# The low part of the logits' products as pairs of half arrays in a stick-breaking attention layer

## The chip, the cores and the metric

The kernel runs on one core of one Trainium2 chip. The metric is the device time of one execution in microseconds (us). Before the change it is 3037.64 us, the median of 3 runs (3036.8 to 3038.7).

## What is computed

One encoder layer on a sequence of 2048 positions with 1024 channels, in float32: a norm, one projection into nine streams of 1024, an attention branch and a convolution branch with gates, a merge, an output projection and a norm at the end. The change lies in the attention: 16 heads of width 64.

```python
scale = 1.0 / math.sqrt(q.shape[-1])
logits = jnp.einsum('bqhd,bkhd->bhqk', qf[:, start:end], kf[:, :end])
mask = s_idx < t_idx
log_not_beta = jnp.where(mask, jax.nn.log_sigmoid(-logits), 0.0)
later = lax.cumsum(log_not_beta, axis=3, reverse=True) - log_not_beta
weights = jnp.where(mask, jnp.exp(jax.nn.log_sigmoid(logits) + later), 0.0)
outs.append(jnp.einsum('bhqk,bkhd->bqhd', weights, vf[:, :end]))
```

A query's weight on a key is the sigmoid of their logit times the product of one minus the sigmoid over all keys between the two.

## The kernel before

**Precision.** Each float32 product is made of float32r products over a split a = hi + lo (split, lines 112 to 114: ScalarE rounds to hi, VectorE subtracts). A projection takes three of them (line 194): hi times hi, hi times lo, lo times hi, over a contraction of 128. A head is only 64 wide, so the logits fit the array's 128 rows in another way: the queries' hi part stands twice in the tile qd, on partitions 0 to 63 and 64 to 127, and the tile k2 holds the keys' hi part on one half of the partitions and their lo part on the other. One product (line 572) gives q_hi k_hi + q_hi k_lo. A second one (line 573) adds q_lo k_hi: the tile ql holds q_lo on the partitions where k2 has the hi part, and zeros, set once at the start (line 512), on the other 64.

**Order of time.** The sequence is reversed, so a query r reads the keys s > r. The queries come in two halves of 1024: half 1 (whose queries have only the keys of their own half) is computed first, then half 0 (all keys). A head's queries go by 256 (a step's two tiles of 128 queries), from the last to the first. In half 1 a step's keys run from its first query to the end; in half 0 there are two steps for each 256 queries, one up to position 1024 (the diagonal piece) and one from there on. Within a step the keys are cut at chunks of 512: segments.

**A step's work.** The items of logits (lines 553 to 583, one for each tile and segment): two products into a PSUM tile lg, of which there are two (pool lgp), a sigmoid by ScalarE into the tile nb (line 575), and, when a tile's last segment is done, a running product along the keys by VectorE, a scan (line 578). Before, all segments of tile 0 come first, then those of tile 1. Then, for each 256 keys, a turn (line 601: TensorE transposes of nb against the identity, and a split into th and tl), and a product with the differences of the values (line 617), emitted two turns later.

**What sets the order.** TensorE executes in the order of emission; the other engines are ordered by the framework. weave_attention (line 643) lists the items of all heads: a logits item stands LEAD = 4 turns ahead of its share of its step's turns, but never more than one step ahead, since nb has NBW = 4 buffers, two for each step. Each item has a cost, an estimate in us of its time on TensorE (0.43 for a logits item of 512 columns), and emit_fill puts pieces of the projection stream (Fill, six products of 512 columns each, cost 1.3) between the items in proportion to the cost that has passed. After the attention, from about 2645 us on, only projections and the output remain.

**Transfers.** All run on the queue of SP. A head's loads are issued in one go by load, at its first logits item: qd (two DMAs for each chunk of queries), ql (one), k2 (two for each chunk of keys) and v2 (one). The weights' loads (line 148) and all others stand on the same queue, in order. The ring st of seven tiles of 128 x 512 stages what goes to and comes from DRAM. The tile dd, the first summand of the diagonal scans, holds the identity and zeros; ident is a tile of its own, and ones a full 128 x 128 tile.

Of the kernel before, what the change touches and what calls it, by code (L numbers as in the profile page):

```python
# [8 lines left out]
F32 = mybir.dt.float32  # L9
F32R = mybir.dt.float32r  # L10
AF = mybir.ActivationFunctionType
# [15 lines left out]
# The weave: buffers of weights, the lead of the logits, and distances and paces in pieces of the projection stream.  # L27
# [27 lines left out]
def layer_kernel(ctx: ExitStack, tc, x, w_in, w_sb, w_cv, w_out, vecs, cw, rows, out):  # L55
    """All sequences are reversed in time: row r is position S-1-r, so that a query r reads
    the keys s > r and the stick is broken in the direction of growing s.

    Every float32 product runs as float32r passes over an exact split a = hi + lo.

    The tensor engine runs in the order of emission: two streams, the attention and the
    projections, are woven so that what one waits for is covered by the other."""
# [5 lines left out]
    ident = const.tile([P, P], F32, name="ident")  # L68
    make_identity(nc, ident)
    ones = const.tile([P, P], F32, name="ones")  # L70
# [21 lines left out]
    def dma(dst, src):  # L92
        """A copy of bytes: float32r has float32's bits."""
        nc.sync.dma_start(out=dst.bitcast(F32) if dst.dtype == F32R else dst,
                          in_=src.bitcast(F32) if src.dtype == F32R else src)
# [20 lines left out]
    def negmean(mr):  # L116
        """-mean * rstd"""
        nm = sm.tile([P, 1], F32, name="nm")
        nc.gpsimd.tensor_scalar(out=nm, in0=mr[:, 0:1], scalar1=mr[:, 1:2], scalar2=-1.0, op0=ALU.mult, op1=ALU.mult)
        return nm  # L120
# [13 lines left out]
    def st(dt=F32):  # L134
        return sg_p.tile([P, CH], dt, name="st", tag="st", bufs=7)
# [4 lines left out]
    # -------------------------------------------------------------- projections, in pieces  # L140
    def load_w(src, col):
        """A block of 128 columns of a weight, [block, partition, kb, column], as hi and lo, contraction on the partitions."""
# [9 lines left out]
    class Fill:  # L152
        """The pieces of the projection stream: (cost in us of the tensor engine, emit)."""
# [21 lines left out]
        def parts(self, src, col, xs, use, *by):  # L175
            """A block: the pieces, per chunk, of out^T[col.., chunk] for each (chunk, acts) of xs; use(chunk, psum, ..) takes
            it, with what the loads `by` have brought. Also the item that loads the weights of the next block."""
# [43 lines left out]
        def pair(self, one, two, first=(), freed=((), ())):  # L221
            """Two blocks, the first chunk of both before the second of either. The items `first` run beside these
            pieces, freed[n] as the activations of chunk n are used up."""
# [28 lines left out]
    def prep(c):  # L252
        """The normed input of chunk c, transposed and split, into xt[c], in pieces."""
# [29 lines left out]
    def xa_tile(to, key):  # L283
        """The next block of a chunk's activations, hi and lo."""
        t = [xa.tile([P, CH], F32R, name=n, bufs=2 * KB) for n in ("xh", "xl")]
        hi, lo = to.setdefault(key, ([], []))
        hi.append(t[0])
        lo.append(t[1])
        return t
# [65 lines left out]
    def even_odd(t):  # L355
        """A row kept as its even and then its odd positions, in the order of the positions."""
        return t.rearrange("p (e n) -> p n e", e=2)

    def block_u(F, m, h):
        """u = c_val * sigmoid(c_gate) of a block of channels."""  # L360
# [23 lines left out]
    # -------------------------------------------------------------- causal depthwise convolution, norm over channels  # L384
# [3 lines left out]
    def conv(m, h, u):  # L388
        """y[r] = sum over d of t[d] u[r+d] + b, with t the taps reversed, on even and odd positions:
        y0 = t0 * (u0 - u1) + (t0 + t1) * u1,  y1 = t1 * (u0+ - u1) + (t0 + t1) * u1."""  # L390
# [39 lines left out]
    def conv_mean(h):  # L430
        """The means over the channels of half h, as items."""
        def mean(c):
# [3 lines left out]
            nc.tensor.matmul(ps, lhsT=ones, rhs=ysum[h][:, :, c % 2 * 256:c % 2 * 256 + 256], start=True, stop=True)  # L436
# [4 lines left out]
    def conv_ln(c):  # L441
        """The norm over the channels of chunk c, the swish and the gate of the branch, as items."""
# [58 lines left out]
    # -------------------------------------------------------------- attention, in items  # L501
    def attention(at, kv, lg_p, pv_p):
        """Summed by parts: with E[r, s] the product of 1 - sigmoid over the keys after r up to s, the weight of s is
        E[r, s-1] - E[r, s], so that o[r] = v[r] + sum over s >= r of E[r, s] (v[s+1] - v[s]), with v[S] = 0."""
        dd = at.tile([P, HALF], F32, name="dd", bufs=1)
        nc.gpsimd.memset(dd, 0.0)
        nc.vector.tensor_copy(out=dd[:, :P], in_=ident)
        sums = {}
        qlo = [[kv.tile([P, CH], F32R, name=f"ql{a}{n}", bufs=1) for n in range(2)] for a in range(2)]
        for a in range(2):  # L510
            for t in qlo[a]:
                nc.gpsimd.memset(t[64 - a * 64:128 - a * 64].bitcast(F32), 0.0)
        zero = at.tile([P, 1], F32, name="zero", bufs=1)
        nc.gpsimd.memset(zero, 0.0)

        def head(i, a, h):
            """The steps of head 2i+a for the queries of half h, each (L items, T/PV items)."""
            k2, v2, qd, ql = {}, {}, {}, {}
            chunks = half(h)

            def load():
                for c in chunks:
# [4 lines left out]
                    ql[c] = qlo[a][c % 2]  # L527
                    dma(ql[c][qs], qdr[c, i][1][qs])
                for c in ([1, 0, 2, 3] if h == 0 else [3, 2]):
                    k2[c] = kv.tile([P, CH], F32R, name="k2", bufs=8)  # L530
                    for e in range(2):
                        dma(k2[c][(a ^ e) * 64:(a ^ e) * 64 + 64], kdr[c, i][e][qs])
# [5 lines left out]
            for qc in (2 * chunks[0] + 1, 2 * chunks[0], 2 * chunks[1] + 1, 2 * chunks[1]):  # L538
# [3 lines left out]
                for pi, (lo, hi) in enumerate(pieces):  # L542
                    steps.append(make_step(i, a, qc, lo, hi, pi == 0, pi == len(pieces) - 1, k2, v2, qd, ql, po, prev,
# [3 lines left out]
        def make_step(i, a, qc, lo, hi, diag, last, k2, v2, qd, ql, po, prev, load):  # L547
# [5 lines left out]
            for j in range(2):  # L553
                s0 = lo + (j * P if diag else 0)
                segs = []
                s = s0
                while s < hi:
                    e = min(hi, (s // CH + 1) * CH)
                    segs.append((s, e))
                    s = e  # L560
                for n, (s, e) in enumerate(segs):
                    def fn(j=j, s0=s0, s=s, e=e, first=(n == 0), end=(n == len(segs) - 1)):
                        if load and first and j == 0:
                            load()
                        if first:
                            tiles[j] = at.tile([P, HALF], F32, name="nb", bufs=NBW)
                        nb = tiles[j]
                        w = e - s
                        kc, ko = s // CH, s % CH
                        js = slice(q * QW + j * P, q * QW + (j + 1) * P)  # L570
                        lg = lg_p.tile([P, CH], F32, name="lg")
                        nc.tensor.matmul(lg[:, :w], lhsT=qd[c][:, js], rhs=k2[kc][:, ko:ko + w], start=True, stop=False)  # L572
                        nc.tensor.matmul(lg[:, :w], lhsT=ql[c][:, js], rhs=k2[kc][:, ko:ko + w], start=False, stop=True)  # L573
                        o = s - s0
                        nc.scalar.activation(nb[:, o:o + w], lg[:, :w], AF.Sigmoid, scale=-QS)  # L575
                        if end:
                            w = hi - s0
                            nc.vector.tensor_tensor_scan(  # L578
                                out=nb[:, :w], data0=nb[:, :w], data1=dd[:, :w] if diag else zero.to_broadcast([P, w]),
                                initial=0.0 if diag else prev[j], op0=ALU.mult, op1=ALU.add)  # L580
                            if not last:
                                prev[j] = nb[:, w - 1:w]
                    items_l.append((0.43 * (e - s) / CH, fn))
# [59 lines left out]
    def weave_attention(steps):  # L643
        """The steps as one list of (cost, emit): the logits run ahead of the transposes, those of the products."""
# [25 lines left out]
    # -------------------------------------------------------------- branch projections, output  # L670
    acts = {}

    def load_acts(key, src, c):
        """The activations of chunk c, split where they land, as items."""
# [7 lines left out]
    def branch(n, h):  # L682
        """A gated branch of the merge for half h: of the attention into pdr, of the convolution into mdr."""
# [29 lines left out]
    def run(F, blks, freed):  # L713
        """The blocks of a half, by pairs at both ends so that one chunk's activations load beside the other's products."""
# [27 lines left out]
    def newest():  # L742
        """The newest instruction of the vector engine."""
# [21 lines left out]
    # -------------------------------------------------------------- the main phase  # L765
# [209 lines left out]
```

## Time and profile before

| what | value |
|---|---|
| median of 3 runs | 3037.64 us |
| span of the profiled execution | 3036.5 us |
| granted TensorE clock, mean | 0.996 |
| PE busy, matmuls | 2959.8 us, 15304 |
| ScalarE busy | 1269.5 us |
| logits, line 572, busy and mean | 246.4 us, 386 ns, 640 products |
| logits, line 573, busy and mean | 233.7 us, 366 ns, 640 products |
| DMA, mean | 150 GB/s |

The span runs from the first to the last instruction of one execution; the time of a run is about 1 us longer. PE is TensorE's matmuls and PEld its weight loads, which run beside them; DVE is VectorE, ACT ScalarE, POOL GpSimd, SPq the queue of SyncE. L573 is line 573 of the kernel. The busy time of PE counts overlapping matmuls with their full durations, and their ends are modelled, so the rate at which TensorE gets through its work is read from the distance of the starts. In a row of a group stand the count, the busy time, the mean in ns, and behind the second bar the idle time of the engine just before these instructions with what ended most of it. A row of the waits has who waited for whom, the total in us, the number of times and the longest. In the timeline a row has the start, the duration, the engine and the line.

### The profile page before, as it was taken

The page shows a single profiled execution, that of the slowest core. Times are in us where ns is not written, and L with a number is a line of the kernel's source. Part 1 is how long each engine was busy: PE and PEld are TensorE (multiplying, and loading weights), DVE is VectorE, ACT ScalarE, POOL GpSimd, SP SyncE. Part 2 cuts the span into 40 slices and gives each one's busy share as a digit, 9 for nine tenths or more (in the row PEclk, how much of TensorE's full clock was granted, in tenths as well). Part 3 has the DMA queues.
Part 4 walks back from the last instruction along what each step waited for, and adds up shares of the span by engine and source line. Part 5 has one row for each costly group of instructions (what it writes and reads, how often), then busy time and mean ns, then how long its engine had stood idle before and what let it go on. Part 6 is the DMA issues. An engine that isn't in the chain of part 4 may idle for free.

```text
span 3036.5 us, 41850 instructions
## 1 busy us (share of the span) xinstructions
PE 2959.8 (97%) x15304; PEld 2484.1 (82%) x15304; DVE 2381.6 (78%) x3175; ACT 1269.5 (42%) x2308; POOL 88.3 (3%) x178
## 2 busy tenths in 40 slices
PE   7999999999999999999999999999999999999998
PEld 6888888888887788888888888887888878878886
DVE  5587787777879888788879888879887788856656
ACT  5333333333336344444445444445445455533222
POOL 1000000000000000000000000000000000000000
PEclk9999999999999999999999999999999999999999
DMA  7543443434434533343335344335545666685552
GB/s 269 172 144 112 148 139 117 149 125 130 139 101 140 169 100 110 114 131 123 111 112 189 103 143 141 99 103 175 164 155 161 191 224 191 208 280 197 161 189 78
DMA packets 260221, 455.92 MB, mean 150 GB/s; under 512 B 30384, under 2 KB 55088, under 8 KB 259888
## 3 DMA queue, kind: packets, MB, share of 16 engines
q1 hardware_dynamic: 260016, 453.25, 46.0%
q8 instruction: 120, 1.97, 0.3%
q14 instruction: 85, 0.70, 0.1%
HBM read 292.70 MB, written 160.43 MB: 149 GB/s over the span
## 4 chain that ended last, share of the span: by engine, by line
PE 73%; DVE 11%; issue 10%; DMA 3%; ACT 2%; POOL 1%; SPq 0%; DVEq 0%; POOLq 0%; ACTq 0%
PE mm L194 52%; PE pv L617 7%; PE tp L601 6%; DVE nb L578 3%; PE lg L573 3%; PE lg L572 3%; DVE tl L114 2%; DVE wlo L114 1%; DVE cy L402 1%; PE mo L900 1%; DMA st<-ydq 1%; DMA ydq<-st 1%; DVE xl L114 1%; DVE st L494 0%; DVE st L493 0%
## 5 line engine op out<-in xcount | busy, mean ns | idle before, releaser
L194 PE MATMUL mm<-xh,whi 128*128 128x512 f32 x2816 | 1144.5, 406 | 1.7 <-ACT whi L113 1.5
L194 PE MATMUL mm<-xh,wlo 128*128 128x512 f32 x2816 | 1110.1, 394 | 1.4 <-DVE wlo L114 1.4
L194 PE MATMUL mm<-xl,whi 128*128 128x512 f32 x2816 | 1106.2, 393 | 1.2 <-DVE xl L114 1.2
L194 PEld LDWEIGHTS mm<-xh,wlo 128*128 128x128 f32 x2816 | 530.0, 188 | 120.9 <-DVE wlo L114 1.9
L194 PEld LDWEIGHTS mm<-xl,whi 128*128 128x128 f32 x2816 | 532.9, 189 | 86.8 <-DVE xl L114 2.4
L194 PEld LDWEIGHTS mm<-xh,whi 128*128 128x128 f32 x2816 | 531.5, 189 | 86.4 <-ACT whi L113 1.9
L113 ACT ACTIVATE th<-tp 128x512 fp32r<-128x512 f32 (+1 forms) x576 | 329.4, 572 | 613.9 <-PE tp L601 606.1
L114 DVE TENSOR_TENSOR tl<-tp,th 128x512 fp32r<-128x512 f32 (+1 forms) x576 | 376.5, 654 | 180.1 <-ACT th L113 178.2
L575 ACT ACTIVATE nb<-lg 128x512 f32<-128x512 f32 (+3 forms) x640 | 334.9, 532 | 308.9 <-PE lg L573 299.0
L578 DVE TENSOR_TENSOR_SCAN nb<-nb,dd 128x256 f32<-128x256 f32 (+7 forms) x256 | 345.1, 1350 | 42.2 <-ACT nb L575 41.5
L601 PE MATMUL tp<-ident,nb 128*128 128x128 f32 x2176 | 337.8, 274 | 20.3 <-DVE nb L578 18.2
L578 DVE TENSOR_TENSOR_SCAN nb<-nb,zero 128x1024 f32<-128x1024 f32 x128 | 300.0, 2346 | 36.5 <-ACT nb L575 36.2
L601 PEld LDWEIGHTS tp<-ident,nb 128*128 128x128 f32 x2176 | 263.4, 140 | 77.9 <-DVE nb L578 22.5
L113 ACT ACTIVATE whi<-wraw 128x512 fp32r<-128x512 f32 x352 | 217.6, 629 | 261.1 <-PE mm L194 238.8
L617 PE MATMUL pv<-tl,v 128*128 128x256 f32 (+1 forms) x1152 | 292.1, 282 | 12.2 <-DVE tl L114 11.6
L114 DVE TENSOR_TENSOR wlo<-wraw,whi 128x512 fp32r<-128x512 f32 x352 | 237.4, 682 | 80.0 <-ACT whi L113 52.9
L617 PE MATMUL pv<-th,v 128*128 128x256 f32 (+1 forms) x1152 | 299.5, 281 | 0.0
L572 PE MATMUL lg<-k,qd 128*128 128x512 f32 (+3 forms) x640 | 246.4, 386 | 11.6 <-ACT nb L575 7.0
L617 PEld LDWEIGHTS pv<-tl,v 128*128 128x128 f32 x1152 | 218.1, 189 | 36.4 <-DVE tl L114 17.2
L573 PE MATMUL lg<-k,ql 128*128 128x512 f32 (+3 forms) x640 | 233.7, 366 | 0.0
L617 PEld LDWEIGHTS pv<-th,v 128*128 128x128 f32 x1152 | 217.8, 189 | 18.5 <-issue 0.2
L402 DVE SCALAR_TENSOR_TENSOR cy<-cu,csum,cy 128x512 f32<-128x512 f32 x240 | 178.1, 742 | 4.4 <-ACT cy L398 0.9
(107 smaller groups left out, 2460.0 us busy)
## 6 DMA issues: line engine op xcount, KB each, us to landing
wraw<-in_w_in SPq DMA_DIRECT2D x288, 256.0 KB, 3.2
k<-kdr SPq DMA_DIRECT2D x192, 128.0 KB, 2.9
v<-vdr SPq DMA_DIRECT2D x96, 256.0 KB, 3.5
kdr<-st SPq DMA_DIRECT2D x64, 256.0 KB, 2.1
qdr<-st SPq DMA_DIRECT2D x64, 256.0 KB, 2.2
qd<-qdr SPq DMA_DIRECT2D x128, 128.0 KB, 2.8
vdr<-st SPq DMA_DIRECT2D x64, 256.0 KB, 2.0
xr<-in_x SPq DMA_DIRECT2D x32, 256.0 KB, 3.8
```

Source lines behind the costliest of these rows:

```text
L113: nc.scalar.activation(hi, src, AF.Copy)
L114: nc.vector.tensor_tensor(out=lo, in0=src, in1=hi.bitcast(F32), op=ALU.subtract)
L194: nc.tensor.matmul(box["ps"], lhsT=l[:, kb], rhs=r[kb], start=(kb == 0 and n == 0), stop=(kb == KB - 1 and n == 2))
L402: nc.vector.scalar_tensor_tensor(out=dst, in0=src[:, j:j + HN], scalar=t, in1=first, op0=ALU.mult, op1=ALU.add)
L572: nc.tensor.matmul(lg[:, :w], lhsT=qd[c][:, js], rhs=k2[kc][:, ko:ko + w], start=True, stop=False)
L573: nc.tensor.matmul(lg[:, :w], lhsT=ql[c][:, js], rhs=k2[kc][:, ko:ko + w], start=False, stop=True)
L575: nc.scalar.activation(nb[:, o:o + w], lg[:, :w], AF.Sigmoid, scale=-QS)
L578: nc.vector.tensor_tensor_scan(out=nb[:, :w], data0=nb[:, :w], data1=dd[:, :w] if diag else zero.to_broadcast([P, w]), initial=0.0 if diag ...
L601: nc.tensor.transpose(out=tp[:, at_:at_ + P], in_=tiles[j][:, so:so + P], identity=ident)
L617: nc.tensor.matmul(o[:, :w], lhsT=lv, rhs=tt[:, o0:o0 + w], start=(diag and t == 0 and n == 0 and e == 0), stop=(last and t == nt - 1 and ...
L900: nc.tensor.matmul(ps, lhsT=a[kb][:, js], rhs=b[:, kb, qs], start=(kb == 0 and n == 0), stop=(kb == KB - 1 and n == 2))
```

## The change

The second product of the logits drops its zero rows. For a segment, the two tiles of queries (j = 0 and 1) are now handled by one item: the first products of both, into both lg tiles; then the second products of both, each over 64 partitions only, tile 0 on one half of the array's rows and tile 1 on the other; then both sigmoids, and, at the step's last segment, both scans. For this, both halves need the keys' hi part: k2 has it on one half of the partitions, and a new tile kx gets it on the other, one tile kx for two chunks (which of the halves is which alternates with the chunk). ql shrinks to the two tiles' columns, packed, each on its half; it is loaded by two DMAs, and needs no zeros. Besides, the ring st has 6 tiles instead of 7, ident becomes the first 128 columns of dd, and ones one column that the one matmul that needs it broadcasts. A logits item has the cost 0.7 for 512 columns of both tiles, where the two items before had 0.86. Comments are dropped.

```diff
-    ident = const.tile([P, P], F32, name="ident")
+    dd = const.tile([P, HALF], F32, name="dd")
+    ident = dd[:, :P]
     make_identity(nc, ident)
-    ones = const.tile([P, P], F32, name="ones")
+    nc.gpsimd.memset(dd[:, P:], 0.0)
+    ones = const.tile([P, 1], F32, name="ones")
...
-        return sg_p.tile([P, CH], dt, name="st", tag="st", bufs=7)
+        return sg_p.tile([P, CH], dt, name="st", tag="st", bufs=6)
...
+        def half_of(a, e, c):
+            x = a ^ e ^ (c % 2)
+            return slice(x * 64, x * 64 + 64)
...
-                    ql[c] = qlo[a][c % 2]
-                    dma(ql[c][qs], qdr[c, i][1][qs])
+                    ql[c] = kv.tile([P, 2, P], F32R, name="ql", bufs=4)
+                    for j in range(2):
+                        dma(ql[c][half_of(a, j, c)], qdr[c, i][1][qs].rearrange("p (q j n) -> p q j n", q=2, j=2)[:, :, j])
...
+                    if c ^ 1 not in kx:
+                        kx[c] = kx[c ^ 1] = kv.tile([P, CH], F32R, name="kx", bufs=4)
                     for e in range(2):
-                        dma(k2[c][(a ^ e) * 64:(a ^ e) * 64 + 64], kdr[c, i][e][qs])
+                        dma(k2[c][half_of(a, e, c)], kdr[c, i][e][qs])
+                    dma(kx[c][half_of(a, 1, c)], kdr[c, i][0][qs])
...
-                        nc.tensor.matmul(lg[:, :w], lhsT=qd[c][:, js], rhs=k2[kc][:, ko:ko + w], start=True, stop=False)
-                        nc.tensor.matmul(lg[:, :w], lhsT=ql[c][:, js], rhs=k2[kc][:, ko:ko + w], start=False, stop=True)
...
+                lgs = [lg_p.tile([P, CH], F32, name="lg") for j in range(2)]
+                for j in range(2):
+                    nc.tensor.matmul(lgs[j][:, :e - ss[j]], lhsT=qd[c][:, q * QW + j * P:q * QW + (j + 1) * P],
+                                     rhs=k2[kc][:, ss[j] - kc * CH:e - kc * CH], start=True, stop=False)
+                for j in range(2):
+                    rows_ = half_of(a, j, c)
+                    kh = k2 if j ^ c % 2 == kc % 2 else kx
+                    nc.tensor.matmul(lgs[j][:, :e - ss[j]], lhsT=ql[c][rows_, q],
+                                     rhs=kh[kc][rows_, ss[j] - kc * CH:e - kc * CH], start=False, stop=True)
...
-                    items_l.append((0.43 * (e - s) / CH, fn))
+            ends = [e for e in range(CH, S + 1, CH) if lo < e <= hi]
+            for n, e in enumerate(ends):
+                items_l.append((0.7 * (e - max(lo, e - CH)) / CH, lambda n=n, e=e: seg(n, e)))
```

More of the change, by code (lines that the diff above doesn't have):

```diff
@@ L435, in mean @@
             ps, mu = mm_p.tile([P, CH], F32, name="mm"), st()
-            nc.tensor.matmul(ps, lhsT=ones, rhs=ysum[h][:, :, c % 2 * 256:c % 2 * 256 + 256], start=True, stop=True)
+            nc.tensor.matmul(ps, lhsT=ones.to_broadcast([P, P]), rhs=ysum[h][:, :, c % 2 * 256:c % 2 * 256 + 256], start=True, stop=True)
             nc.scalar.activation(mu, ps, AF.Copy)
@@ L502, in attention @@
     def attention(at, kv, lg_p, pv_p):
-        dd = at.tile([P, HALF], F32, name="dd", bufs=1)
-        nc.gpsimd.memset(dd, 0.0)
-        nc.vector.tensor_copy(out=dd[:, :P], in_=ident)
         sums = {}
[L509 to L512, printed above, removed]
         zero = at.tile([P, 1], F32, name="zero", bufs=1)
         nc.gpsimd.memset(zero, 0.0)
+        def half_of(a, e, c):
+            x = a ^ e ^ (c % 2)
+            return slice(x * 64, x * 64 + 64)
         def head(i, a, h):
-            k2, v2, qd, ql = {}, {}, {}, {}
+            k2, v2, qd, ql, kx = {}, {}, {}, {}, {}
             chunks = half(h)
@@ L542, in head, with make_step @@
                 for pi, (lo, hi) in enumerate(pieces):
-                    steps.append(make_step(i, a, qc, lo, hi, pi == 0, pi == len(pieces) - 1, k2, v2, qd, ql, po, prev,
+                    steps.append(make_step(i, a, qc, lo, hi, pi == 0, pi == len(pieces) - 1, k2, kx, v2, qd, ql, po, prev,
                                            load if not steps else None))
             return steps
-        def make_step(i, a, qc, lo, hi, diag, last, k2, v2, qd, ql, po, prev, load):
+        def make_step(i, a, qc, lo, hi, diag, last, k2, kx, v2, qd, ql, po, prev, load):
             c, q = qc // 2, qc % 2
@@ L552, in make_step @@
             items_l = []
[L553 to L582, printed above, removed]
-                    items_l.append((0.43 * (e - s) / CH, fn))
@@ new lines, in from_, with seg @@
+            def from_(j):
+                return lo + (j * P if diag else 0)
+            def seg(n, e):
+                if load and n == 0:
+                    load()
+                if n == 0:
+                    for j in range(2):
+                        tiles[j] = at.tile([P, HALF], F32, name="nb", bufs=NBW)
+                kc = (e - 1) // CH
+                ss = [max(from_(j), kc * CH) for j in range(2)]
+                lgs = [lg_p.tile([P, CH], F32, name="lg") for j in range(2)]
+                for j in range(2):
+                    nc.tensor.matmul(lgs[j][:, :e - ss[j]], lhsT=qd[c][:, q * QW + j * P:q * QW + (j + 1) * P],
+                                     rhs=k2[kc][:, ss[j] - kc * CH:e - kc * CH], start=True, stop=False)
+                for j in range(2):
+                    rows_ = half_of(a, j, c)
+                    kh = k2 if j ^ c % 2 == kc % 2 else kx
+                    nc.tensor.matmul(lgs[j][:, :e - ss[j]], lhsT=ql[c][rows_, q],
+                                     rhs=kh[kc][rows_, ss[j] - kc * CH:e - kc * CH], start=False, stop=True)
+                for j in range(2):
+                    nb, s0 = tiles[j], from_(j)
+                    nc.scalar.activation(nb[:, ss[j] - s0:e - s0], lgs[j][:, :e - ss[j]], AF.Sigmoid, scale=-QS)
+                    if e == hi:
+                        w = hi - s0
+                        nc.vector.tensor_tensor_scan(
+                            out=nb[:, :w], data0=nb[:, :w], data1=dd[:, :w] if diag else zero.to_broadcast([P, w]),
+                            initial=0.0 if diag else prev[j], op0=ALU.mult, op1=ALU.add)
+                        if not last:
+                            prev[j] = nb[:, w - 1:w]
```

## The prediction

> **What bounds the kernel now.** I read the page first: the busy times, the slices, the chain that ended last.
>
> ```profile
> span 3036.5 us, 41850 instructions
> ...
> PE 2959.8 (97%) x15304; PEld 2484.1 (82%) x15304; DVE 2381.6 (78%) x3175; ACT 1269.5 (42%) x2308; POOL 88.3 (3%) x178
> ...
> PE   7999999999999999999999999999999999999998
> ...
> DVE  5587787777879888788879888879887788856656
> ...
> PE 73%; DVE 11%; issue 10%; DMA 3%; ACT 2%; POOL 1%; SPq 0%; DVEq 0%; POOLq 0%; ACTq 0%
> ```
>
> TensorE is at 9 tenths in every slice but the first and the last, and the chain lies on it for 73%. VectorE is the next engine, mostly at 7 to 9 tenths while the attention runs. Then the waits of PE, longest first:
>
> ```profile
> PE tp L601 <- DVE nb L578: 18.2, 15, 3.2
> PE tp L275 <- DVE xr L266: 12.3, 1, 12.3
> PE pv L617 <- DVE tl L114: 11.6, 13, 1.9
> PE lg L572 <- ACT nb L575: 7.0, 8, 2.1
> ```
>
> All four together are 49 us of 3036. So PE executes its stream nearly without holes, and an instruction taken out of the stream is worth its spacing to the next one, as long as VectorE's 78% doesn't take over. Spacing is not the duration in the groups, because matmuls overlap. The timeline around 1506 us shows the difference, and how the weight loads stand to the matmuls:
>
> ```profile
> 1505.73 0.59 PEld L601 LDWEIGHTS tp<-ident,nb 128*128 128x128 f32 x4
> 1505.96 0.60 PE L601 MATMUL tp<-ident,nb 128*128 128x128 f32 x4
> ...
> 1506.31 0.47 PE L194 MATMUL mm<-xh,whi 128*128 128x512 f32 x1
> ...
> 1506.62 0.39 PE L194 MATMUL mm<-xl,whi 128*128 128x512 f32 x1
> ...
> 1507.54 0.39 PE L194 MATMUL mm<-xh,wlo 128*128 128x512 f32 x1
> 1507.54 0.19 PEld L572 LDWEIGHTS lg<-k,qd 128*128 128x128 f32 x1
> ...
> 1507.77 0.39 PE L572 MATMUL lg<-k,qd 128*128 128x512 f32 x1
> 1507.78 0.19 PEld L573 LDWEIGHTS lg<-k,ql 128*128 128x128 f32 x1
> 1508.00 0.39 PE L573 MATMUL lg<-k,ql 128*128 128x512 f32 x1
> 1508.00 0.19 PEld L194 LDWEIGHTS mm<-xh,whi 128*128 128x128 f32 x1
> 1508.23 0.40 PE L194 MATMUL mm<-xh,whi 128*128 128x512 f32 x1
> ```
>
> A matmul over 512 columns lasts 0.39 us but the next starts 0.23 us after it. Among products each weight load starts with the matmul ahead of it, so one load is always done ahead, never two. Every matmul of the trace reads 128*128: it has no half array.
>
> **The saving.** The changed instruction is L573, the queries' low part.
>
> ```profile
> L573 PE MATMUL lg<-k,ql 128*128 128x512 f32 x448 | 176.9, 395 | 0.0
> ```
>
> From the loops, a head has 6 segments (a step's keys within one chunk of 512) for the queries of half 1 and 14 for those of half 0; 16 heads each make 320 segments of two tiles, 640 products. The 512 wide are the row's 448; the other 192 are 64 each of 384, 256 and 128 columns. In a segment the two products run on different halves of the array, so where they overlap fully the narrower costs nothing. The narrower ones are, per head, 2+10 of 512 columns, 2+2 of 384 and 2+2 of 128: 192, 64 and 64 in all. The spacing of narrow products comes from L617:
>
> ```profile
> 1509.63 0.28 PE L617 MATMUL pv<-th,v 128*128 128x256 f32 x1
> 1509.75 0.28 PE L617 MATMUL pv<-tl,v 128*128 128x256 f32 x1
> 1509.87 0.22 PE L617 MATMUL pv<-th,v 128*128 128x128 f32 x1
> 1509.93 0.27 PE L617 MATMUL pv<-tl,v 128*128 128x128 f32 x1
> ```
>
> 256 columns take 0.12, 128 take 0.06; 384 lies between 0.12 and 0.23, so 0.17. The saving is at most 192 x 0.23 + 64 x 0.17 + 64 x 0.06 = 44.2 + 10.9 + 3.8 = 59 us, or 0.184 us per segment. That is the whole prize: 1.9% of the span. (The 366 ns mean of the groups would make it look twice as large.)
>
> **What the halves cost on PE.** Three prices, each paid once per segment, and none is in the trace.
>
> *The trail of the second half.* A load of 128 columns that isn't hidden can be priced from the four transposes: from their first start to the second L194 after them is 1506.62 - 1505.96 = 0.66; without the first L194's 0.23 that is 0.43, or 0.11 each, where a 128-column product with its load hidden takes 0.06. So a bare load is 0.05. If the second half's load starts with the first half's matmul, as every load here starts with the matmul ahead of it, the pair trails by 0.05. Bounds: 0 (both loads fit in the 0.23 of the product ahead: 2 x 0.05) and 0.05. I take 0.05, because no row shows two loads ahead: 320 x 0.05 = 16 us. The Trainium skill, "TensorE: Matmul & The Clock Gate", section "Measured speedup vs the span model", adds about 4 ns per further tile of a pack; by that, an estimate, the trail would be 1.3 us, and nothing here shows it.
>
> *The two changes of shape*, from whole to half and back. The nearest change in the trace is from transposes to products: 0.66 = 4 x 0.11 + 0.23 leaves nothing over. That is the lower end, 0. The upper end is that a change waits until the array is empty: 0.39 - 0.23 = 0.16 after the last column, and then the load behind it is bare too, 0.05: 0.21 a change, 0.42 a segment, 134 us. I take one bare load a segment, 0.05, or 16 us, for it is nearer to the row that shows a change of kind without any loss than to one that shows an empty array, which none does. Below nothing it can't go: no instruction leaves with it. The Trainium skill, "TensorEngine Tiling (Array Packing)", section "Key Properties", says that changing the tiling mode, not just the tile, drains TensorE; no row here can show it, and what it would make of the time is the rival below.
>
> **What else moves.** *Both buffers of the logits at once.* A segment now takes both PSUM tiles lg, and the next one needs both back. After the last column the sigmoid starts about 0.20 us later and takes 0.60:
>
> ```profile
> 1502.49 0.39 PE L573 MATMUL lg<-k,ql 128*128 128x512 f32 x1
> ...
> 1502.92 0.60 ACT L575 ACTIVATE nb<-lg 128x512 f32<-128x512 f32 x1
> ```
>
> (1502.49 + 0.23 = 1502.72.) So the second tile is free 0.20 + 2 x 0.60 = 1.4 us after the segment and the next segment's second product needs it 0.23 after its first. Following weave_attention's rule, segments follow each other directly about 1.1 times in a head of half 1 and 2.1 times in one of half 0, some 50 times; otherwise a turn or a product pair lies between. Even between direct neighbours emit_fill puts one or two pieces of 6 x 0.23 = 1.4 us. So the cover is 1.4 + 0.23 against 1.4, thin only if ScalarE has a queue. Bounds: 0, and 50 waits of 0.9 (the 7.0 us over 8 waits above), 44. I take +5.
>
> *The scans.* Both scans of a step now come behind its last segment, together:
>
> ```profile
> L578 DVE TENSOR_TENSOR_SCAN nb<-nb,zero 128x1024 f32<-128x1024 f32 x128 | 300.0, 2346 | 36.5 <-ACT nb L575 36.2
> L573 PE MATMUL lg<-k,ql x640: 273/393/632, 73.5 to 2644.8; 128*128 128x512 f32 x96, 128*128 128x256 f32 x64
> ```
>
> A head has 10 turns in half 1 and 26 in half 0, 576 in all, and the row of L573 spans 2571 us: 4.5 us a turn. The last segment of a four-turn step stands two turns ahead of its transposes (before: the last tile's stood one ahead): 8.9 us against 0.2 + 1.2 + 4.7 = 6.1. Covered, with 2.8 to spare where 1.4 was. But 4.7 us of scan in one piece delay the splits behind it on VectorE's queue, for which L617 waits. The 11.6 us of that wait could double; the earlier last segment could as well take some of L601's 18.2. I book +3 for these, for the transfers and for the smaller ring together, between -10 and +20.
>
> *Transfers.* load issues 16 instead of 12 DMAs for a head of half 1, 24 instead of 18 for one of half 0: 160 more, all on SP, behind which the weights queue.
>
> ```profile
> SPq L148 <- DVE wlo L114: 458.9, 232, 14.8
> ...
> 1508.88 0.32 SPq L94 DMA_DIRECT2D kdr<-st  x1
> ...
> q1 hardware_dynamic: 260016, 453.25, 46.0%
> ```
>
> Six more issues of 0.32 are 1.9 us once per head. SP itself stands waiting 459 us at the weights' loads, because their buffers are still in use, so it is early by more than that. kx adds 96 x 128 KB = 12.6 MB, under 3% of the bytes. If the cover were gone, 1.9 x 32 = 61 us would show; PE's list has next to no wait on weights, so nothing.
>
> *The ring st loses one of 7 tiles.* Nothing among PE's waits above comes from it; the staging loads of the last 400 us are what it would delay, and they run a block ahead. In the +3. *Start:* POOL loses 2 us of clearing ql and has the clearing of dd moved ahead; both lie in its idle time, before 4.4 us, and PE's first wait is for VectorE's xr (12.3 above). Nothing.
>
> **Sum.** -59 + 16 + 16 + 5 + 3 = -19. The profiled execution's span is 3036.5, and the median 3037.6 lies 1.1 above it (start and end around the span); so 3036.5 - 19 + 1.1 = 3018.6, say 3018. Its own range: PE's cost from one bare load in all to three (16 to 48) and the rest from 0 to 20 gives -43 to +9: 2995 to 3047, most of it below 3031. What a measurement of this kernel can tell from no change is about 0.2%, 6 us.
>
> **Rivals.**
>
> *The change of shape empties the array.* This ends on the other side. Place: before the first half product and before the first whole one after it. Price: from half of the empty time and three bare loads (2 x 0.08 + 0.15 = 0.31) to all of it (2 x 0.16 + 0.15 = 0.47); 99 to 150 us against the 59, with +8 for the rest: 3086 to 3138, and it decides from 0.16 a segment (0.184 less 8 / 320) on. For it: a matmul does last 0.39, and nothing here shows a half array started behind a whole one. Against: transposes and products change places once per turn, 576 times, at no loss. Chance 0.24, in which shorter emptyings with results from 3040 to 3086 are counted. By the rule on drains of the Trainium skill, "TensorEngine Tiling (Array Packing)", section "Key Properties", this is the outcome; how long a drain is that page doesn't tell.
>
> *Everything overlaps.* Both loads go ahead, no change costs: -59 + 8 = -51, 2986. For it: loads are hidden everywhere else among products. Against: one load ahead at most. Chance 0.08.
>
> *The halves don't run side by side.* The change doesn't do what it says: the second product starts after the first's columns, 0.23 later. Nothing saved, 0 to 32 us of changes, +8: 3046 to 3078. No row speaks for or against. Chance 0.06.
>
> *The gain goes into waits.* PE gets its 27 us and gives them back at L572 (both lg tiles out) and at L601 and L617 (VectorE at 8 tenths). It takes 50 waits of 0.4 us more than booked. For it: L575's 299 us of ScalarE waiting show it is usually ready, which speaks against; VectorE's 8 and 9 tenths speak for. 3031 to 3044. Chance 0.12.
>
> ```profile
> ACT nb L575 <- PE lg L573: 299.0, 274, 2.6
> ```
>
> **From cases to numbers.** The forecast has 0.50, the rivals 0.24, 0.08, 0.06 and 0.12. Of the forecast's share 0.47 ends below 3031 and 0.03 above; of the emptying array's 0.02 within 6 us and 0.22 beyond; the gain lost in waits gives 0.02, 0.08 and 0.02 to the three sides. Faster by over 0.2%: 0.47 + 0.08 + 0.02 = 0.57. Within: 0.03 + 0.08 + 0.02 = 0.13. Slower: 0.22 + 0.06 + 0.02 = 0.30. The range from 2985 to 3080 leaves out over half of the emptying array (0.14) and under half of the full overlap (0.03).
>
> **What would show it.** In the changed profile: the two low products of a segment as rows of 64*128, started 0.00 to 0.05 apart, and the next product 0.23 after the second; 0.23 apart is the rival without overlap. From the second high product to the first low one 0.23 to 0.28 is my forecast, 0.35 or more the emptying. Waits of L572 on L575 over 20 us, or of L601 and L617 on VectorE beyond 50 us, are the fourth rival. PE's busy time says little, as it adds overlapped durations. I am wrong in the main if a segment's four products take as long as the 0.92 us of four whole ones.

## The result and the profile after

The changed kernel takes 3131.88 us, the median of 4 runs (3127.95 to 3135.06), against 3038.17 before; the ratio is 1.0307, with a 95% interval from 1.0292 to 1.0321. It is 94 us slower. The page of its profile, for the rows shown of before:

```profile
span 3131.1 us, 42139 instructions
...
PE 3033.5 (97%) x15304; PEld 2426.8 (78%) x15304; DVE 2381.7 (76%) x3174; ACT 1265.2 (40%) x2308; POOL 90.7 (3%) x174
...
PE 72%; DVE 11%; issue 10%; DMA 3%; ACT 2%; POOL 1%; SPq 0%; DVEq 0%; POOLq 0%; ACTq 0%
```

Nothing in it looks different: the same count of matmuls, the same 97%, the same chain. The low products, by form, are half arrays, and last longer than the whole ones did (0.40 us):

```profile
L578 PE MATMUL lg<-k,ql 64*128 64x512 f32 x256 | 127.4, 498 | 0.0
...
L578 PE MATMUL lg<-kx,ql 64*128 64x512 f32 x192 | 95.5, 498 | 0.0
```

The timeline of one segment answers to the one shown of before:

```profile
1516.32 0.62 PE L573 MATMUL lg<-k,qd 128*128 128x512 f32 x2
...
1516.87 0.18 PEld L578 LDWEIGHTS lg<-kx,ql 64*128 64x128 f32 x1 [0.36 <-issue]
1516.87 0.50 PE L578 MATMUL lg<-kx,ql 64*128 64x512 f32 x1
1516.87 0.18 PEld L578 LDWEIGHTS lg<-k,ql 64*128 64x128 f32 x1
1516.88 0.49 PE L578 MATMUL lg<-k,ql 64*128 64x512 f32 x1
...
1517.30 0.19 PEld L196 LDWEIGHTS mm<-xh,whi 128*128 128x128 f32 x1 [0.24 <-issue]
1517.30 0.50 PE L196 MATMUL mm<-xh,whi 128*128 128x512 f32 x1
...
1517.64 0.39 PE L196 MATMUL mm<-xl,whi 128*128 128x512 f32 x1
```

The two halves do start together, 0.01 apart. But from the second high product (1516.32 + 0.23 = 1516.55) to them it is 0.32 instead of 0.23; neither load was done ahead; from them to the next product it is 0.43, and from that to the one after 0.34. From the first high product to the second one behind the segment: 1517.64 - 1516.32 = 1.32, where five whole products took 5 x 0.23 = 1.15. In this segment of 512 columns the halves cost 0.17 after their saving of 0.23, so 0.40 before it.

The waits of PE:

```profile
PE pv L627 <- DVE tl L116: 21.0, 20, 2.6
PE tp L277 <- DVE xr L268: 12.7, 2, 11.7
PE lg L573 <- ACT nb L582: 10.0, 13, 2.9
PE tp L611 <- DVE nb L585: 10.0, 7, 2.3
PE tp L611 <- DVE tl L116: 8.6, 8, 2.7
```

All rows of this list together make 87 us; those of the same list before made 66. What the page does not say is whether the 94 us are the halves, or the order of work that came with them.

### The profile page after: what moved, and what is told of

Same layout as the page of the kernel before. It is cut to its first block, busy times and chain, and to the rows that moved or that the text cites. A ratio compares the mean times of both kernels' runs of the same rounds, so it can differ in the third digit from the quotient of the medians.

```text
span 3131.1 us, 42139 instructions
## 1 busy us (share of the span) xinstructions
PE 3033.5 (97%) x15304; PEld 2426.8 (78%) x15304; DVE 2381.7 (76%) x3174; ACT 1265.2 (40%) x2308; POOL 90.7 (3%) x174
## 4 chain that ended last, share of the span: by engine, by line
PE 72%; DVE 11%; issue 10%; DMA 3%; ACT 2%; POOL 1%; SPq 0%; DVEq 0%; POOLq 0%; ACTq 0%
PE mm L196 51%; PE pv L627 7%; PE tp L611 6%; DVE nb L585 4%; PE lg L573 3%; PE lg L578 3%; DVE tl L116 1%; DMA st<-ydq 1%; DVE wlo L116 1%; DVE cy L404 1%; PE mo L910 1%; DMA xr<-in_x 1%; DVE st L492 0%; ACT nb L582 0%; DVE st L496 0%
## 5 line engine op out<-in xcount | busy, mean ns | idle before, releaser
L196 PE MATMUL mm<-xh,whi 128*128 128x512 f32 x2816 | 1175.3, 417 | 3.9 <-DVE st L711 2.4
L582 ACT ACTIVATE nb<-lg 128x512 f32<-128x512 f32 (+3 forms) x640 | 309.7, 532 | 267.7 <-PE lg L578 253.2
L585 DVE TENSOR_TENSOR_SCAN nb<-nb,dd 128x256 f32<-128x256 f32 (+7 forms) x256 | 334.7, 1345 | 46.2 <-ACT nb L582 45.1
L611 PE MATMUL tp<-dd,nb 128*128 128x128 f32 x2176 | 336.3, 274 | 18.7 <-DVE nb L585 10.0
L611 PEld LDWEIGHTS tp<-dd,nb 128*128 128x128 f32 x2176 | 266.3, 141 | 78.8 <-DVE tl L116 11.6
L627 PE MATMUL pv<-th,v 128*128 128x256 f32 (+1 forms) x1152 | 308.7, 289 | 2.4 <-ACT th L115 2.4
L573 PE MATMUL lg<-k,qd 128*128 128x512 f32 (+3 forms) x640 | 191.0, 378 | 15.4 <-ACT nb L582 10.0
L404 DVE SCALAR_TENSOR_TENSOR cu<-cd,cwt,cu 128x512 f32<-128x512 f32 x240 | 179.1, 746 | 3.2
```

The costliest lines, as they stand in the source:

```text
L196: nc.tensor.matmul(box["ps"], lhsT=l[:, kb], rhs=r[kb], start=(kb == 0 and n == 0), stop=(kb == KB - 1 and n == 2))
L404: nc.vector.scalar_tensor_tensor(out=dst, in0=src[:, j:j + HN], scalar=t, in1=first, op0=ALU.mult, op1=ALU.add)
L573: nc.tensor.matmul(lgs[j][:, :e - ss[j]], lhsT=qd[c][:, q * QW + j * P:q * QW + (j + 1) * P], rhs=k2[kc][:, ss[j] - kc * CH:e - kc * CH], ...
L582: nc.scalar.activation(nb[:, ss[j] - s0:e - s0], lgs[j][:, :e - ss[j]], AF.Sigmoid, scale=-QS)
L585: nc.vector.tensor_tensor_scan(out=nb[:, :w], data0=nb[:, :w], data1=dd[:, :w] if diag else zero.to_broadcast([P, w]), initial=0.0 if diag ...
L611: nc.tensor.transpose(out=tp[:, at_:at_ + P], in_=tiles[j][:, so:so + P], identity=ident)
```

## The experiments

The diffs are shortened: operands that do not matter are left out. Theory A: the changes of shape. By the segment above, 320 x 0.40 = 128 us, less the 59 saved: 69, and the rest follows from the holes. Theory B: pairing the tiles, the smaller ring and the added DMAs carry most of it.

**The halves undone, everything else kept** (e1).

```diff
-  lhsT=ql[c][rows_, q], rhs=kh[kc][rows_, ss[j] - kc * CH:e - kc * CH]
+  lhsT=ql[c][:, q], rhs=kh[kc][:, ss[j] - kc * CH:e - kc * CH]
```

> The changed kernel with one thing undone: the low products are read over all 128 partitions again (weights ql[:, q], keys k2 or kx whole), so every matmul is 128*128; order of the products, kx, the DMAs, the ring of six and the costs stay. It adds the low part of both tiles, and the keys' low part, to each logit, so its numbers are others, not its work. Theory A (each change of the array's shape empties it: 0.095 us on entry, 0.195 on leaving and 0.106 for the bare load behind, 0.40 a segment, 127 us, against 59 saved): 3132 - 69 = 3063, or down to 3040 if the remaining 25 us come from the holes too. Theory B (pairing, the smaller ring and the added DMAs cost most of the 94 us): 3105 or more.

Measured: 3086.8 us, 1.0152 of before (1.0135 to 1.0169). Between the theories: the halves are worth 45 us of the 94, and 48 are there without any half array. Neither theory alone holds. (The four runs of e1 lie from 3078.6 to 3095.3, so this division is good to several us only.)

**What the halves cost by themselves.** In e2, each low product stands behind its own high product, four changes of shape a segment:

```diff
   for j in range(2):
       matmul(lgs[j], lhsT=qd[c] ..., start=True, stop=False)
-  for j in range(2):
       rows_ = half_of(a, j, c)
```

> The changed kernel with the order high 0, low 0, high 1, low 1 in each segment: four changes of shape instead of two, and no pair side by side. Theory A: twice 0.40 a segment and nothing saved: 3132 + 127 + 59 = 3318. Theory B: only the lost overlap, 3132 + 59 = 3191.

Measured: 3262.5, 131 us more than the changed kernel.

In e3, both low products use one half of the rows:

```diff
-  rows_ = half_of(a, j, c)
-  kh = k2 if j ^ c % 2 == kc % 2 else kx
+  rows_ = half_of(a, 0, c)
+  kh = k2 if c % 2 == kc % 2 else kx
```

> The changed kernel with both low products of a segment on the same half of the rows: still two changes of shape, but nothing side by side. Tile 1 takes tile 0's low part, so its numbers are others. If the pair does overlap in full, as starts 0.003 us apart say: 3132 + 59 = 3191. If the overlap is only in the records: 3132.

Measured: 3178.5, 47 more. The overlap is real. Its timeline has a segment's two low products in one row, and 0.65 from their start to the next product, where the pair side by side needed 0.43:

```profile
1516.19 0.62 PE L573 MATMUL lg<-k,qd 128*128 128x512 f32 x2
1516.74 0.72 PE L578 MATMUL lg<-kx,ql 64*128 64x512 f32 x2
1517.39 0.50 PE L196 MATMUL mm<-xh,whi 128*128 128x512 f32 x1
```

In e4, the pair is executed twice:

```diff
-  for j in range(2):
+  for n_, j in enumerate((0, 1, 0, 1)):
       rows_ = half_of(a, j, c)
```

> The changed kernel with the pair of low products executed twice in a row in each segment (the low part counts double): four half products, still two changes of shape. Theory A, cost per stay: only the second pair's columns, 147456 x 0.45 ns = 66 us: 3132 + 66 = 3198. If each half product pays, or the loads between the pairs are bare: 0.1 to 0.4 more a segment, 3230 to 3325.

Measured: 3202.3, 70 more. So the price is paid for a stay in the other shape and not for a product. The timeline takes it apart further:

```profile
1500.76 0.49 PE L578 MATMUL lg<-kx,ql 64*128 64x512 f32 x1
...
1500.77 0.49 PE L578 MATMUL lg<-k,ql 64*128 64x512 f32 x1
...
1501.10 0.39 PE L578 MATMUL lg<-kx,ql 64*128 64x512 f32 x1
1501.10 0.39 PE L578 MATMUL lg<-k,ql 64*128 64x512 f32 x1
1501.42 0.19 PEld L196 LDWEIGHTS mm<-xh,whi 128*128 128x128 f32 x1 [0.36 <-issue]
1501.42 0.49 PE L196 MATMUL mm<-xh,whi 128*128 128x512 f32 x1
```

The first pair is followed after 0.34, the second, the last in its shape, after 0.32. In the changed kernel one pair is both first and last: 0.43 = 0.23 + 0.11 + 0.09. So a change of shape costs 0.09 behind the last product of the old shape and 0.11 at the first of the new one, 0.20 each way. The 0.11 is a bare load: the load starts together with its product, which lasts 0.49 instead of 0.39. The 0.09 I read as the array emptying; that name is argued, the time is measured.

In e7 the kernel before gets 320 half products of zeros by 64 columns:

```diff
+  if j == 0:
+      matmul(lg[:, :64], lhsT=ql[c][ls, js], rhs=k2[kc][ls, ko:ko + 64], start=False, stop=False)
```

> The kernel before with one more product in each segment, for tile 0 only, between its high and its low product: 64 rows of zeros by 64 columns of keys, a half array that adds nothing to the sum. 320 stays in the other shape with hardly any columns, 0.03 us each. Theory A: 320 x (0.40 + 0.03) = 138 us more, 3176. If a change of shape were free: 3048.

Measured: 3145.0, 106 us more than before, for next to no columns. Its timeline around one stay:

```profile
1504.67 0.39 PE L572 MATMUL lg<-k,qd 128*128 128x512 f32 x1
1504.99 0.29 PE L574 MATMUL lg<-k,ql 64*128 64x64 f32 x1
1505.22 0.50 PE L575 MATMUL lg<-k,ql 128*128 128x512 f32 x1
1505.55 0.39 PE L572 MATMUL lg<-k,qd 128*128 128x512 f32 x1
```

0.32 + 0.23 + 0.33 = 0.88 instead of 0.46: the stay costs 0.42, 0.03 of it columns. 320 times that is 134; 106 arrived. The same in e2, where 131 arrived of 186, though its timeline shows the price unchanged: from the first product of a segment to the second one behind it 1505.91 - 1503.98 = 1.93, two stays of 0.39 over the 1.15. The slower TensorE waits less for the others: all PE's waits together are 45 us in e7 against 66 before, and 48 in e2 against 87 in the changed kernel. The one for the splits in e2:

```profile
PE pv L626 <- DVE tl L116: 6.2, 9, 1.6
```

That is 6.2 us, against 21.0 in the changed kernel. Nor do 69 and 48 add up to 117, but to 94; how far the waits explain that is said at the end, with the sum.

**Where the other 48 us come from.** e5 and e6 bring single parts of the change into the kernel before: the ring, and the pairing.

```diff
-  return sg_p.tile([P, CH], dt, name="st", tag="st", bufs=7)
+  return sg_p.tile([P, CH], dt, name="st", tag="st", bufs=6)
```

> The kernel before with the ring st of six tiles instead of seven, nothing else. Theory A: no wait of TensorE on the ring, 3038 within 6. Theory B (the ring carries part of the 25 us that the changes of shape leave over): 3044 to 3063.

Measured: 3044.8, 1.0020 of before (1.0010 to 1.0029): 6 us, at the lower edge of theory B.

```diff
-  items_l.append((0.43 * (e - s) / CH, fn))
+  for j in range(2):
+      matmul(lgs[j], lhsT=ql[c][:, q * QW + j * P:q * QW + (j + 1) * P], rhs=k2[kc], start=False, stop=True)
...
+  items_l.append((0.86 * (e - max(lo, e - CH)) / CH, lambda n=n, e=e: seg(n, e)))
```

(seg is that of the change, but for the low products shown here.)

> The kernel before with the logits' items paired as in the changed one (both high products, both low ones, both sigmoids, both scans together; cost 0.86 for 512 columns, so the fill is spread as before), with whole arrays, ql with its zeros, seven tiles in the ring and no kx. Theory A: 3038, or up to 3050 through both lg tiles being out at once. Theory B: 3060 and more, with waits of line 573's successor on the sigmoid.

Measured: 3095.7, 1.0186 (1.0169 to 1.0203). The pairing alone, with whole arrays, costs 57 us. With the ring's 6 that is more than the 48 of e1, which has both; e1 also books its items at 0.7 instead of 0.86 and loads ql and kx in the changed way, and no run takes these apart. I had looked for it at the sigmoids; the waits of PE put it elsewhere:

```profile
PE pv L620 <- DVE tl L114: 36.8, 36, 3.1
PE tp L275 <- DVE xr L266: 11.6, 1, 11.6
PE tp L604 <- DVE nb L578: 6.8, 7, 2.8
PE lg L568 <- ACT nb L575: 6.4, 12, 0.8
```

The wait for the lg tiles stays at 6.4 us (7.0 before), while the product with the values waits 36.8 for the split on VectorE (11.6 before). The timeline of VectorE in the changed kernel has both scans in one row, and the next split only behind them and three shorter operations:

```profile
1985.39 4.59 DVE L585 TENSOR_TENSOR_SCAN nb<-nb,zero 128x1024 f32<-128x1024 f32 x2 [1.17 <-ACT nb L582]
1989.90 0.66 DVE L641 TENSOR_TENSOR og<-pv,st 64x512 f32<-64x512 f32 x1
1990.48 1.28 DVE L116 TENSOR_TENSOR wlo<-wraw,whi 128x512 fp32r<-128x512 f32 x2
1991.69 0.68 DVE L116 TENSOR_TENSOR tl<-tp,th 128x512 fp32r<-128x512 f32 x1
```

Theory C says that the scans keep the splits waiting, theory D that it is something else in the pairing. Cutting the scans at the segments is to tell them apart, in the kernel before (e8, in its own names), with pairs (e9) and in the changed kernel (e10):

```diff
-  if e == hi:
-      tensor_tensor_scan(out=nb[:, :w], ..., initial=0.0 if diag else prev[j])
+  tensor_tensor_scan(out=nb[:, o:w], ..., initial=nb[:, o - 1:o] if o else 0.0 if diag else prev[j])
```

> The kernel before with the scan of a tile cut at its segments: one scan of at most 512 columns right after each sigmoid, started from the last column of the one before; 640 scans instead of 384, each cut about 0.09 us (2 x 1.22 against 2.35), 22 us more on VectorE in all. Theory C (long scans on VectorE's queue are what TensorE waits for in this kernel): the 18 and 12 us of waits on nb and tl shrink, 3010 to 3035. Theory D (they are not): 3037 to 3045.

Measured: 3029.6, 0.9971 of before (0.9958 to 0.9984): faster by 0.3%, some 10 us, the one version here that beats both kernels. From its waits of PE:

```profile
PE pv L616 <- DVE tl L114: 19.7, 28, 1.8
...
PE lg L572 <- ACT nb L575: 5.9, 7, 2.9
```

The wait of the transposes for the scans, 18.2 before, is 1.5 here; that for the splits, which theory C said would shrink, has risen by 8.

> The kernel with paired items and whole arrays (3096), its scans cut at the segments in the same way: two of at most 1.2 us in a row instead of two of 2.35. Theory C (the pairing costs its 57 us because two scans, 4.7 us, stand in a row ahead of the splits): 3040 to 3055. Theory D (both lg tiles out at once, two sigmoids in a row, or the fill spread in larger portions): 3085 or more.

Measured: 3056.8, 1.0056 (1.0041 to 1.0071): 39 us less than with whole scans. The cut gains some 10 us in the kernel before too, so like against like the pairing costs 27 us with cut scans (3056.8 against 3029.6), where it cost 57 with whole ones. About half of its price hangs on the length of the scans, and half does not: neither theory alone holds.

> The changed kernel with the scans cut at the segments. Theory C: the cost of the pairing goes and the changes of shape stay, 3039 + 6 for the ring + 45 to 69: 3090 to 3114. Theory D: 3125 or more.

Measured: 3095.9: 36 us better than the changed kernel, inside theory C's range, and 66 above the kernel before with the same cut.

Is it that two scans stand in a row? e11 has the pairs with whole scans, but tile 1's as an item of its own:

```diff
+  items_l.append((0, lambda: scan(1)))
```

> The kernel with paired items and whole arrays (3096), with uncut scans, but that of tile 1 is an item of its own, one place later in the list of the logits' items. Theory C: the splits get in between, 3040 to 3060. Theory D: 3085 or more.

Measured: 3102.8, 1.0210 (1.0193 to 1.0227), no better than e6. But this does not test that form of theory C, for the edit hardly parted the scans: on VectorE 142 of the 192 pairs of them still stand directly one behind the other, against 163 in e6 and 15 in the kernel before. A row of its VectorE, and its longest wait of PE:

```profile
1964.72 4.59 DVE L559 TENSOR_TENSOR_SCAN nb<-nb,zero 128x1024 f32<-128x1024 f32 x2 [0.25 <-ACT nb L584]
```

```profile
PE pv L625 <- DVE tl L114: 45.6, 44, 3.8
```

Last, e12 alternates the tiles in the kernel before, without pairing them. Theory F is that the order does it, with tile 0's scan moved to the end of a step's items; theory E that it is handing over two tiles at one place.

```diff
+  k_ = len(items_l) // 2
+  items_l = [items_l[x * k_ + y] for y in range(k_) for x in range(2)]
```

> The kernel before with only the order of a step's logits items changed: segment 0 of tile 0, segment 0 of tile 1, segment 1 of tile 0, and so on, each still an item of its own with its cost and its place. As with the pairs, tile 0's scan now comes at the end of the step's items, next to tile 1's; unlike with the pairs, no two tiles are handed over at one place. Theory F (the pairing costs its time because no scan can start until the step's last items): 3080 or more. Theory E (because two tiles' products, sigmoids and scans come at one place): 3040 to 3055.

Measured: 3064.0, 1.0076 (1.0058 to 1.0094): 23 us, between the two. Here it is the transposes that wait for the scans, 27.1 us where it was 18.2:

```profile
PE tp L604 <- DVE nb L578: 27.1, 22, 3.7
PE pv L620 <- DVE tl L114: 15.3, 20, 2.0
```

So the order alone, in which no scan starts before the end of a step's items, costs about 23 us in the kernel before. They cannot simply be counted as part of the pairing's 57: in e12 the transposes' wait for the scans is what grew, and with the pairs (e6) that wait fell to 6.8. What in the pairing weighs how much (two scans in a row, two sigmoids together, coarser portions of the projections between the items) stays open, beyond the half that goes with the length of the scans.

## Why the prediction was wrong

**The saving** was right: the pair runs side by side, and undoing that costs 47 us where 59 were counted, while PE's waits shrink by 13 (87 us in all in the changed kernel, 74 in e3).

**The trail** was mis-sized and didn't matter: 0.01 at most instead of 0.05, so about 3 us or less instead of 16. The rule of the Trainium skill, "TensorE: Matmul & The Clock Gate", section "Measured speedup vs the span model", of about 4 ns per tile, agrees with these starts (1516.87 and 1516.88).

**The two changes of shape** are the step that failed. I took 16 us, one bare load a segment, and the runs show 0.40 a segment, 128 us. A segment's four products take 0.98 (1517.30 - 1516.32), over the 0.92 that I had named as the sign of being wrong in the main. My own upper end, 0.21 a change, had the sum, by errors that cancel: the emptying is 0.09 rather than 0.16, the bare load 0.11 rather than 0.05, together 0.20. I chose the lower end by the nearest row, transposes to products; but that row only changes the kind of work, not the shape of the array, and says nothing on this. That it "leaves nothing over" was bound to come out, too: the 0.11 a transpose had been taken from the same 0.66, and the rows show the first product behind the transposes with 0.47 instead of 0.39 and the next one 0.31 after it. (The single transposes do start 0.11 apart, so the sum holds; it was no evidence.) The Trainium skill, "TensorEngine Tiling (Array Packing)", section "Key Properties", said that a change of mode drains TensorE; the trace agrees, with 0.09 us that I read as the emptying and the bare load behind it. The rival "the change of shape empties the array" held in its mechanism and in the deciding point of 0.16 a segment, but I had given it 0.24. That the time lies in its 3086 to 3138 is in part luck: with the measured 0.40 and its +8 for the rest it comes to 3115.

**The waits** are the second failure. I booked +8 for the lg tiles, the scans, the transfers and the ring together; all but the halves costs 48 (e1). The lg tiles, my +5, cost little (7.0 us of waiting before, 10.0 after). The long scans carry about half of the pairing's price (e9), and I had argued them covered, with 2.8 us to spare, because I compared a scan's end with its own step's transposes. In e6 the transposes' wait for the scans even fell, from 18.2 to 6.8 us; what rose was the other one that I named and left small, that for the splits of earlier turns, which stand behind 4.6 us of scan among other things. The ring's 6 us were in the +3 with the rest.

**The sum** as it would have to read: -59 + 128 = 69 for the halves and 48 for the rest are 117, and 23 of them did not arrive. Part of the 23 is in the count of the halves: the low product of a narrow segment was worth more than its 0.06. With 256 and 128 columns the stretch to the second product behind the segment takes 0.70 in e1 (from 130.34) and 0.91 in the changed kernel (from 133.81), where 0.40 - 0.06 would be 0.34 more. The medians of this difference, over the segments without a wait, are 0.17, 0.22 and 0.23 for the 192, 64 and 64 segments by width, which makes about 60 us instead of 69. Of the other 14, PE's waits carry 8 (95 us in all in e1, 87 in the changed kernel). What is left, 6, lies within the scatter of e1.

## What to carry to other kernels

Running half-filled products as two half arrays pays only if the stay in the other shape saves more than its fixed price, here 0.40 us a round trip against 0.23 for one pair of 512 columns. By these numbers two pairs for each stay would be the least, and PSUM would have to have room for them; no run here tries it. Price a change of state on an engine by rows that show that very change, and where there are none, let the worse bound weigh as much as the better one. When work is regrouped, look behind the moved instruction in its engine's queue: long operations handed over together delay the short ones that somebody else waits for, and cutting them can be worth as much as what one was after: cut scans gained some 10 us in the kernel before and 36 to 39 where they came in pairs, against the forecast of 19.

## What the hardware showed besides

A wait of TensorE can cost more than its length. In the changed kernel a wait of 4.31 us is followed by products 0.43 apart instead of 0.23:

```profile
935.44 1.01 PE L277 MATMUL tp<-dd,xr 128*128 128x128 f32 x4 [4.31 <-DVE tl L116]
...
936.67 0.63 PE L196 MATMUL mm<-xl,whi 128*128 128x512 f32 x1
937.10 0.63 PE L196 MATMUL mm<-xh,wlo 128*128 128x512 f32 x1
```

The granted clock of that stretch is in the table by windows, in the column before the DMA's share:

```profile
935.00:939.00 4.00, 3.56 (x11) 2.88 (x12) 2.87 (x5) 3.34 (x6) 0.00 (x0) 0.57 0.34 131
```

Over the whole span the mean granted clock is 0.996 before, 0.991 after, 0.990 in e6 and 0.996 in e8. 0.005 of 3131 is 16 us of full clock. That waits bring such stretches on fits this and the Trainium skill ("TensorE: Matmul & The Clock Gate", "What's actually happening": half clock after an idle window of about 3.4 us), but no run changed the clock alone, so what it carries can only be estimated: at most the span times what is missing from a clock of 1. That is 12 us before and 31 in e6, 19 more; all PE's waits together are 66 and 101, 35 more. The two make 54 of the 57 us by which e6's span is longer (3093.6 against 3036.5). In the same way e1 has 29 of waits and 25 of clock for its 57, and e12 14 and 12 for its 26. By this estimate, what the pairing and the order cost is time in which TensorE waits, or runs at the lower clock; the work itself does not get longer.
